# Decoder block on one Trainium2 core: how the key/value banks are emptied, when a gate vector is loaded, and which queue issues some stores

## The chip, the cores and the metric

The kernel runs on one core of one Trainium2 chip. A core has TensorE (PE, matrix products into PSUM banks, with a weight load PEld that overlaps them), VectorE (DVE), ScalarE (ACT), GpSimd (POOL) and SyncE (SP), and 16 DMA engines. Each engine works through its own queue of instructions in order. A DMA is issued by an instruction in the queue of some engine; its transfer then runs beside the engines. The metric is the device time of one execution in microseconds (us), the median of several runs.

## The reference, cut to what matters

One decoder layer over 2048 tokens of width 1024, in fp32. The part that the change touches is the combined projection and what is made of it:

```
h = modulate(rms_norm(x, g_pre_mix), shift_m, scale_m)
proj = h @ w_in
q_a, k_a, v_a, q_m, k_m, v_m, o_m, i_m, f_m, g_a, g_m = split(proj)   # 512 128 128, 4 x 512, 4 4, 2 x 1024
q_a, k_a = rope(q_a, positions), rope(k_a, positions)
y_a = sliding_window_attention(q_a, k_a, v_a, sinks)      # window 128, 8 query heads, 2 key/value heads
y_m = sigmoid(o_m) * head_layer_norm(mlstm_chunkwise(...))
mix = (sigmoid(g_a) * (y_a @ w_branch_attn) + sigmoid(g_m) * (y_m @ w_branch_mlstm)) @ w_out
x = x + gate_m * rms_norm(mix, g_post_mix)
h2 = modulate(rms_norm(x, g_pre_ffn), shift_f, scale_f)
x = x + gate_f * rms_norm((silu(h2 @ w_gate) * (h2 @ w_up)) @ w_down, g_post_ffn)
```

## The kernel before

Every fp32 product is made of three products of a rounded part and a remainder ("hi" and "lo"): ScalarE casts an operand to its hi part (L259 for weights, L1348 in paired products), VectorE subtracts to get the lo part (L260, L1349), and PE multiplies hi by hi, hi by lo and lo by hi (L204). Some large products are paired after Strassen and Winograd, with seven products for eight.

The 2048 tokens are cut into four blocks of 512, each of four subtiles of 128 tokens, and two blocks make a superblock. For a superblock the order of the work is: q and key/value projection of its first block (`q_kv`), attention, the mLSTM value projection (`vm`) of both blocks, `q_kv` and attention of the second block, then pairs for mLSTM q and k, output gate and branch gates, and the outputs. So `q_kv` ends in a key/value group at four places: once before a `vm` group and once before the first pair, in each superblock. The FFN follows (`program2`).

A projection of a block is a `token_group` (L310): four PSUM banks named `acc`, one for each subtile. The weights come in pieces; the last piece finishes the banks one after the other, and `evac(t, ps)` empties each. There are four `acc` banks in all, so that the next group's first matmul for a subtile can't start before the bank has been read by everything that reads it. Four more banks, `mix`, serve transposes and smaller products.

The key/value group is 264 columns wide: 128 of k, 128 of v, 8 gate preactivations (i and f). `evac_kv` reads its bank five times: VectorE adds the gate biases (L801, L802), ScalarE copies v into a buffer (L804), VectorE subtracts the previous subtile's v, `v_last`, from it (L805; the attention product over two neighbouring key tiles uses v and a difference), and `rope` (L746) copies k with ScalarE (L751). Between them ScalarE copies the new `v_last` (L806), which waits for L805. The two stores of v and of the difference go to `at_d` in HBM (L808, L810), from which attention loads them. `rope` multiplies and adds on VectorE (L759 to L763); for k the last addition (L763) is on GpSimd. The stream of a q or k subtile then waits a set delay and transposes, splits and stores (`q_stream` L766, stores L775; `k_stream` L788).

Temporary buffers named `tx` come from one pool of nine (L103), `tm` from another of nine (L106). A new tile waits until all users of the old one, a store from it too, are done.

The order of the instructions on each engine isn't written out by hand. The program issues them in its own order with set delays for the small streams, and the Tile scheduler places them by times of its own; after that the order on each engine is fixed. All DMAs are issued by SP's queue, so a store there stands until its data is made, and later loads stand behind it. Each DMA signals one of eight completion semaphores, which are given out in turn over all queues in the scheduled order; an issue waits for the DMA that had its semaphore before.

The other lines that the change touches: the normalized rows after the mixer (`norm_out` store L561, `residual_out` store L588), the mLSTM value store L823, the attention output store L970 and the mLSTM output store L1089 (a hi and a lo part each), the output gate store L1150, the branch gate store L1160 (where ScalarE has made the stored copy), and `load_gg` (L1809), which loads the vector that scales the FFN's result, at the start of `program2` (L1814). The FFN's first residual sums read the layer's stored rows and L1426 and L1429 build the operands of its first pairs.

Of the kernel before, what the change touches and what calls it, by code (L numbers as in the profile page):

```python
# [10 lines left out]
F32 = mybir.dt.float32  # L11
# [4 lines left out]
ALU = mybir.AluOpType  # L16
# [3 lines left out]
P = 128  # L20
S = 2048
D = 1024
KD = D // P
TB = 512
NT = TB // P
# [6 lines left out]
HQ, HKV, HD = 8, 2, 64  # L32
GQ = HQ // HKV
# [38 lines left out]
def decoder_block(ctx: ExitStack, tc: tile.TileContext, a: dict, out: bass.AP, dbg=None):  # L72
    nc = tc.nc
# [29 lines left out]
    def tx(shape, dtype=F32):  # L103
        return tpool.tile(shape, dtype, tag="tx", name=nm("tx"), bufs=9)
# [106 lines left out]
    def spawn(gen, delay=0.0):  # L211
        st = [now[0] + delay, gen, False]
        streams.append(st)
        return st
# [340 lines left out]
    def norm_out(xy, t, dst_n, sx):  # L555

        V.tensor_tensor(sx[:, 0:1], sx[:, 0:1], sx[:, 1:2], op=ALU.add)
        r = rsqrt_of_sumsq(sx[:, 0:1], 1)
        for xr, y0, c in xy:
            A.activation(y0, xr, AF.Copy, scale=r[:, 0:1])  # L560
            nc.sync.dma_start(dst_n[t * P:(t + 1) * P, c], y0)  # L561

    def residual_out(nk, lhs, w, keep, resid, gg, dst, dst_n):


        st = {}

        def rest(t, y, r):
            ys = (st["keep"][:, t, :], y)
            cs = [slice(h2 * 512, (h2 + 1) * 512) for h2 in range(2)]  # L570
            if dst_n is not None:
                yield L_REST[0] + L_REST[1] * t
            xs = [resid(t, c) for c in cs]
            if dst_n is not None:
                yield L_REST[2]
            sx = small.tile([P, 2], F32, tag="sx", name=nm("sx"), bufs=4)
            for h2 in range(2):
                V.scalar_tensor_tensor(xs[h2], ys[h2], r[:, 0:1], xs[h2], op0=ALU.mult, op1=ALU.add)
                nc.sync.dma_start(dst[t * P:(t + 1) * P, cs[h2]], xs[h2])
                if dst_n is not None:  # L580
                    A.activation(ys[h2], xs[h2], AF.Square, accum_out=sx[:, h2:h2 + 1])
            if dst_n is not None:
                V.tensor_tensor(sx[:, 0:1], sx[:, 0:1], sx[:, 1:2], op=ALU.add)
                r2 = rsqrt_of_sumsq(sx[:, 0:1], 1)
                yield L_REST[3]
                for h2 in range(2):
                    A.activation(ys[h2], xs[h2], AF.Copy, scale=r2[:, 0:1])
                    nc.sync.dma_start(dst_n[t * P:(t + 1) * P, cs[h2]], ys[h2])  # L588

        def evac(hf, t, ps):  # L590
            if not st:
                st["ss"] = small.tile([P, 8], F32, tag="ss8", name=nm("ss8"), bufs=2)
                st["keep"] = keep([NT, 512])
            ss = st["ss"]
            y = st["keep"][:, t, :] if hf == 0 else tm([P, 512])
            A.activation(y, ps, AF.Square, accum_out=ss[:, hf * 4 + t:hf * 4 + t + 1])
            V.tensor_tensor(y, ps, gg(slice(hf * 512, (hf + 1) * 512)), op=ALU.mult)
            if hf == 0:
                return
            s = small.tile([P, 1], F32, tag="ss1", name=nm("ss1"), bufs=4)  # L600
            V.tensor_tensor(s, ss[:, t:t + 1], ss[:, 4 + t:5 + t], op=ALU.add)
            g = rest(t, y, rsqrt_of_sumsq(s, 1, 4.0 * EPS))
            if dst_n is not None:
                spawn(g, next(g))
            else:
                for _ in g:
                    pass

        for hf in range(2):
            yield from token_group(srcs_rows(w, nk, hf * 512), nk, 512, lhs, lambda t, ps, hf=hf: evac(hf, t, ps))  # L610
# [125 lines left out]
    def superblock(sb):  # L736
        b0, b1 = 2 * sb, 2 * sb + 1
        R = {}
# [4 lines left out]
            return lhs  # L743


        def rope(ps, heads, b, t):  # L746
            sin, cos = tables[sb]
            t += (b % 2) * NT
            W = heads * HD
            raw = tx([P, W])  # L750
            A.copy(raw, ps[:, :W])  # L751
            src = raw.rearrange("p (h u f) -> p h u f", u=2, f=32)
            cb = cos[:, t, :].unsqueeze(1).to_broadcast([P, heads * 2, 32])
            sb_ = sin[:, t, :].unsqueeze(1).to_broadcast([P, heads, 32])
            y = tx([P, W])
            z = tx([P, W])
            zz = z.rearrange("p (h u f) -> p h u f", u=2, f=32)
            yy = y.rearrange("p (h u f) -> p h u f", u=2, f=32)
            V.tensor_tensor(y.rearrange("p (h f) -> p h f", f=32), raw.rearrange("p (h f) -> p h f", f=32), cb, op=ALU.mult)  # L759
            V.tensor_tensor(zz[:, :, 0, :], src[:, :, 1, :], sb_, op=ALU.mult)  # L760
            V.tensor_tensor(zz[:, :, 1, :], src[:, :, 0, :], sb_, op=ALU.mult)
            V.tensor_tensor(yy[:, :, 0, :], yy[:, :, 0, :], zz[:, :, 0, :], op=ALU.subtract)
            (G if heads == HKV else V).tensor_tensor(yy[:, :, 1, :], yy[:, :, 1, :], zz[:, :, 1, :], op=ALU.add)  # L763
            return y

        def q_stream(b, t, y):  # L766
            yield L_ROPE
            pt = mix_tile()
            for j in range(GQ):
                transpose(pt[:, j * P:(j + 1) * P], y[:, j * P:(j + 1) * P])  # L770
            hi, lo = tx([P, 512], F32R), tx([P, 512], F32R)
            A.activation(hi, pt, AF.Copy, scale=HD ** -0.5)
            V.scalar_tensor_tensor(lo, pt, HD ** -0.5, hi.bitcast(F32), op0=ALU.mult, op1=ALU.subtract)
            for i, q in enumerate((hi, lo)):
                nc.sync.dma_start(at_d[b * NT + t][:, i * 512:(i + 1) * 512], q.bitcast(F32))  # L775

        R["qk"] = []

        def evac_q(b):
            return lambda t, ps: R["qk"].append(spawn(q_stream(b, t, rope(ps, HQ, b, t))))  # L780

        def load_kv():
            raw = raw_tile([KD, 264])
# [14 lines left out]

        def evac_kv(b):
            def evac(t, ps):  # L800
                V.tensor_tensor(gt[:, t, 0:4], ps[:, 256:260], b_if[:, 0:4], op=ALU.add)  # L801
                V.tensor_tensor(gt[:, t, 32:36], ps[:, 260:264], b_if[:, 4:8], op=ALU.add)  # L802
                va = tx([P, 2, P])
                A.copy(va[:, 0, :], ps[:, 128:256])  # L804
                V.tensor_tensor(va[:, 1, :], ps[:, 128:256], v_last, op=ALU.subtract)  # L805
                A.copy(v_last, va[:, 0, :])  # L806
                n = b * NT + t
                nc.sync.dma_start(at_d[n][:, AT_V + P:], va[:, 1, :])  # L808
                if n + 1 < S // P:
                    nc.sync.dma_start(at_d[n + 1][:, AT_V:AT_V + P], va[:, 0, :])  # L810
                R["qk"].append(spawn(k_stream(b * NT + t, rope(ps, HKV, b, t))))
            return evac

        def q_kv(b):
# [4 lines left out]
        def vm(b):  # L819
            def evac(t, ps):  # L820
                v = tx([P, 512])
                A.copy(v, ps)
                nc.sync.dma_start(vm_d[b][:, t, :], v)  # L823
            yield from token_group(srcs_rows(w_in, KD, C_VM), KD, 512, lhs_h(b), evac)


# [63 lines left out]
        def attention(n):  # L890
# [76 lines left out]
            A.copy(yh, yps)  # L967
            V.tensor_tensor(yl, yps, yh.bitcast(F32), op=ALU.subtract)
            for i, y in enumerate((yh, yl)):
                nc.sync.dma_start(y_d[b][:, i, :, t * P:(t + 1) * P], y.bitcast(F32).rearrange("p (j q) -> p j q", j=GQ))  # L970

        ready = [0]

# [63 lines left out]
        def chunk_out(c):  # L1037
# [48 lines left out]
            A.copy(yh, om)  # L1086
            V.tensor_tensor(yl, om, yh.bitcast(F32), op=ALU.subtract)
            for i, y in enumerate((yh, yl)):
                nc.sync.dma_start(y_d[b][:, 2 + i, :, cs], y.bitcast(F32))  # L1089

        outs = []

# [51 lines left out]
        def done_om(p):  # L1144
            def done(qd, v, in_psum):
                f, b = 2 * p + int(qd[0]) - 1, b0 + int(qd[1]) - 1
                u = plain() if in_psum else v
                A.activation(u, v, AF.Tanh, scale=0.5)
                A.activation(u, u, AF.Identity, scale=om_s[:, f:f + 1], bias=om_s[:, f:f + 1])
                nc.sync.dma_start(om_d[b][:, f, :], u)  # L1150
            return done

        def done_gate(i, p):
            def done(qd, v, in_psum):
                f, b = 2 * p + int(qd[0]) - 1, b0 + int(qd[1]) - 1
                u = v
                if in_psum:
                    u = plain()
                    A.copy(u, v)
                nc.sync.dma_start(g_d[b][:, i, f, :], u)  # L1160
            return done

        def in_pair(kind, p):
# [167 lines left out]
    F = {}  # L1331
# [466 lines left out]
    def program():  # L1798
# [7 lines left out]
        yield lambda: next(phase2)  # L1806
        yield from items[last:]

    def load_gg():  # L1809
        F["gg"] = F["pool"].tile([P, D], F32, name="gg_f")  # L1810
        nc.sync.dma_start(F["gg"], gg_f_d)

    def program2():
        yield load_gg  # L1814
        for b2 in range(NB2):
            yield from gate_up(b2)
            yield from down(b2)

    phase2 = run2(program2())
# [31 lines left out]
```

## Time and profile before

| what | value |
|---|---|
| median of 3 runs | 2741.42 us (2739.41 to 2742.02) |
| profiled execution, own time | 2741.79 us |
| profiled execution, span from first to last instruction | 2740.1 us |
| mean granted PE clock | 0.988 of full speed |
| instructions | 35791 |
| moved by DMA | 513.99 MB, 188 GB/s on average |

The profile gives for each engine its busy time and share of the span. Views of the trace group instructions by the kernel's line, the tile written and the tiles read; `acc<-big,hl` at L204 is a matmul into an `acc` bank. Where a row ends in brackets, as `[8.55 <-ACT tx L751]`, the engine stood idle for that long before the instruction, and what ended it is named: here ScalarE's instruction of L751 that wrote a `tx` tile. An "x4" is four instructions in a row.

A view of stretches gives, for each span of time, the busy time of each engine, the clock that PE was granted (1.00 is full speed) and the share of the DMA engines' time that was used. The trace shows four long waits of PE for L751, at about 86, 208, 776 and 896 us.

### The profile page before, as it was taken

To read this page: it belongs to the slowest core of one execution; us is meant where nothing else is said; L and a number is where in the kernel's file an instruction comes from. 1 tells how busy PE (TensorE), PEld (TensorE's weight loads), DVE (VectorE), ACT (ScalarE), POOL (GpSimd) and SP (SyncE) were. 2 spreads that over 40 slices of the span, in tenths; PEclk is the share of its full clock that TensorE was granted. 3 is DMA by queue.
4 is the path that set the end of the run, shared out by engine and by line. 5 is a ranking of instruction groups with operands and counts; after the bars stand their busy time and mean duration, and the time that the engine had idled before them with its cause. 6 is when DMAs were issued, how large, how long until landed. Compare 5 with 4: busy or idle time off the path is not lost.

```text
span 2740.1 us, 35791 instructions
## 1 busy us (share of the span) xinstructions
PE 2646.6 (97%) x12310; PEld 2139.0 (78%) x12310; DVE 1995.3 (73%) x3922; ACT 1292.4 (47%) x2542; POOL 158.6 (6%) x205
## 2 busy tenths in 40 slices
PE   6898999999989899999998999999999999999998
PEld 4666788888876668888887888888877888888886
DVE  7959877767785988876586767776677766766466
ACT  5646644445754564344563433334554333333444
POOL 2010002100101000110000000000000000000000
PEclk9999999999999999999999999999999999999999
DMA  6655445687674545568755654446675323324566
GB/s 247 232 173 166 139 142 174 212 330 257 218 239 126 199 154 159 185 219 304 255 195 197 198 179 161 147 157 204 208 261 192 116 98 102 108 97 141 183 214 215
DMA packets 355223, 513.99 MB, mean 188 GB/s; under 512 B 25297, under 2 KB 213837, under 8 KB 349921
## 3 DMA queue, kind: packets, MB, share of 16 engines
q1 hardware_dynamic: 355040, 511.71, 56.3%
q8 instruction: 97, 1.59, 0.2%
q14 instruction: 86, 0.70, 0.1%
HBM read 358.17 MB, written 145.06 MB: 184 GB/s over the span
## 4 chain that ended last, share of the span: by engine, by line
PE 80%; DVE 7%; DMA 6%; issue 4%; ACT 2%; SPq 0%; POOL 0%; DVEq 0%; POOLq 0%; ACTq 0%
PE acc L204 57%; PE mix L204 22%; PE mix L209 2%; DVE hl L1349 1%; DVE tm L428 1%; DMA raw<-in_w_ffn_down_dram 1%; DMA big<-big 1%; DMA tx<-in_w_ada_dram 1%; DMA big<-g_d 1%; ACT hl L1348 1%; DVE wlo L260 0%; DMA raw<-as_d 0%; DMA at<-at_d 0%; DMA big<-in_x_dram 0%; ACT tm L941 0%
## 5 line engine op out<-in xcount | busy, mean ns | idle before, releaser
L204 PE MATMUL acc<-big,hl 128*128 128x512 f32 x3936 | 949.5, 395 | 14.9 <-ACT tx L751 13.1
L204 PEld LDWEIGHTS acc<-big,hl 128*128 128x128 f32 x3936 | 735.8, 189 | 184.3 <-ACT tx L751 13.5
L1348 ACT CAST hl<-raw 128x512 fp32r<-128x512 f32 x732 | 440.2, 621 | 488.4 <-PE acc L204 226.7
L1349 DVE TENSOR_TENSOR hl<-raw,hl 128x512 fp32r<-128x512 f32 x732 | 497.9, 696 | 195.9 <-ACT hl L1348 195.4
L204 PE MATMUL acc<-whi,big 128*128 128x512 f32 (+1 forms) x1280 | 382.7, 378 | 22.8 <-ACT tx L751 15.0
L204 PE MATMUL mix<-big,hl 128*128 128x512 f32 x1232 | 334.0, 393 | 8.1 <-DVE big L1429 7.0
L204 PEld LDWEIGHTS acc<-whi,big 128*128 128x128 f32 x1280 | 234.9, 190 | 72.5 <-ACT tx L751 15.9
L204 PEld LDWEIGHTS mix<-big,hl 128*128 128x128 f32 x1232 | 231.7, 188 | 59.9 <-DVE big L1429 7.5
L204 PE MATMUL acc<-wlo,big 128*128 128x512 f32 (+1 forms) x640 | 240.6, 378 | 4.6 <-DVE wlo L260 4.5
L204 PE MATMUL acc<-hl,hl 128*128 128x512 f32 x1008 | 237.0, 393 | 4.3 <-DVE hl L1349 2.4
L204 PEld LDWEIGHTS acc<-hl,hl 128*128 128x128 f32 x1008 | 187.0, 188 | 49.6 <-DVE hl L1349 7.9
L204 PE MATMUL mix<-hl,hl 128*128 128x512 f32 x792 | 183.2, 391 | 2.4 <-ACT hl L1348 1.6
L204 PEld LDWEIGHTS mix<-hl,hl 128*128 128x128 f32 x792 | 147.9, 188 | 36.8 <-ACT hl L1348 3.5
L260 DVE TENSOR_TENSOR wlo<-raw,whi 128x1024 fp32r<-128x1024 f32 (+1 forms) x96 | 110.3, 1149 | 76.1 <-ACT whi L259 70.1
L204 PE MATMUL acc<-big,whi 128*128 128x512 f32 x512 | 155.0, 391 | 1.2 <-ACT whi L259 1.2
L259 ACT CAST whi<-raw 128x1024 fp32r<-128x1024 f32 (+1 forms) x96 | 94.3, 984 | 120.6 <-PE acc L204 116.1
L204 PEld LDWEIGHTS acc<-wlo,big 128*128 128x128 f32 x640 | 122.7, 192 | 28.1 <-DVE wlo L260 6.2
L475 POOL TENSOR_TENSOR rs<-ms,nhalf 128x1 f32<-128x1 f32 (+1 forms) x56 | 42.1, 764 | 1650.6 <-DVE ms L473 1518.7
L204 PE MATMUL acc<-hcT2h,hl 128*128 128x512 f32 x352 | 118.1, 396 | 1.5 <-ACT w L1492 1.5
L204 PE MATMUL mix<-hcT4h,hl 128*128 128x512 f32 x352 | 117.3, 394 | 0.0
L204 PEld LDWEIGHTS acc<-big,whi 128*128 128x128 f32 x512 | 95.6, 188 | 21.2 <-ACT whi L259 1.7
L204 PE MATMUL acc<-big,wlo 128*128 128x512 f32 x256 | 96.4, 392 | 0.1
(333 smaller groups left out, 3392.7 us busy)
## 6 DMA issues: line engine op xcount, KB each, us to landing
raw<-in_w_in_dram SPq DMA_DIRECT2D x48, 1024.0 KB
as_d<-w SPq DMA_DIRECT2D x154, 256.0 KB
raw<-as_d SPq DMA_DIRECT2D x70, 512.0 KB
raw<-in_w_ffn_gate_dram SPq DMA_DIRECT2D x22, 1024.0 KB
raw<-in_w_ffn_up_dram SPq DMA_DIRECT2D x22, 1024.0 KB
raw<-ws_d SPq DMA_DIRECT2D x40, 512.0 KB
tx<-in_w_ada_dram SPq DMA_DIRECT2D x64, 256.0 KB
y_d<-tm SPq DMA_DIRECT2D x64, 256.0 KB
```

What stands on the lines that cost most here:

```text
L204: T.matmul(o, lhsT=lhsT, rhs=rhs, start=start, stop=stop, skip_group_check=resumed)
L209: T.transpose(o, i, ident[:k, :k])
L259: A.copy(hv, src)
L260: V.tensor_tensor(lv, src, hv.bitcast(F32), op=ALU.subtract)
L428: V.scalar_tensor_tensor(acc, raw[:, k, :], c_, acc, op0=ALU.mult, op1=ALU.add)
L475: G.tensor_tensor(r[:, :n], ms[:, :n], nhalf[:, :n], op=ALU.pow)
L1348: A.copy(v(hi), src)
L1349: V.tensor_tensor(v(lo), src, v(hi).bitcast(F32), op=ALU.subtract)
```

## The change

- `evac_kv` copies the whole bank, 264 columns, with one ScalarE operation into a buffer of 392 columns. All else reads that buffer: rope, the subtraction (into the last 128 columns), the gate additions. `v_last` is now copied by VectorE. The two stores read the same buffer. `rope` takes a buffer in place of a bank, and its last addition is on VectorE for k too. `evac_q` makes the copy that `rope` made.
- Stores of what ScalarE has just written are issued by ScalarE's queue (`nc.scalar`) in place of SP's: 128 of them in an execution, by source line 8 (L561), 24 (L588), 16 each of L775, L823, L970, L1089 and L1150, and 16 of L1160's 64. Of a hi and lo pair the hi part moves; the lo part, made by VectorE, stays on SP.
- The gate vector's tile is still placed at the start of `program2`, and its load is yielded after the first `gate_up`.

```diff
         for xr, y0, c in xy:
             A.activation(y0, xr, AF.Copy, scale=r[:, 0:1])
-            nc.sync.dma_start(dst_n[t * P:(t + 1) * P, c], y0)
+            nc.scalar.dma_start(dst_n[t * P:(t + 1) * P, c], y0)
...
-        def rope(ps, heads, b, t):
+        def rope(raw, heads, b, t):
             sin, cos = tables[sb]
             t += (b % 2) * NT
             W = heads * HD
-            raw = tx([P, W])
-            A.copy(raw, ps[:, :W])
+            raw = raw[:, :W]
...
-            (G if heads == HKV else V).tensor_tensor(yy[:, :, 1, :], yy[:, :, 1, :], zz[:, :, 1, :], op=ALU.add)
+            V.tensor_tensor(yy[:, :, 1, :], yy[:, :, 1, :], zz[:, :, 1, :], op=ALU.add)
...
             for i, q in enumerate((hi, lo)):
-                nc.sync.dma_start(at_d[b * NT + t][:, i * 512:(i + 1) * 512], q.bitcast(F32))
+                (nc.scalar, nc.sync)[i].dma_start(at_d[b * NT + t][:, i * 512:(i + 1) * 512], q.bitcast(F32))
...
         def evac_q(b):
-            return lambda t, ps: R["qk"].append(spawn(q_stream(b, t, rope(ps, HQ, b, t))))
+            def evac(t, ps):
+                raw = tx([P, 512])
+                A.copy(raw, ps)
+                R["qk"].append(spawn(q_stream(b, t, rope(raw, HQ, b, t))))
+            return evac
...
         def evac_kv(b):
             def evac(t, ps):
-                V.tensor_tensor(gt[:, t, 0:4], ps[:, 256:260], b_if[:, 0:4], op=ALU.add)
-                V.tensor_tensor(gt[:, t, 32:36], ps[:, 260:264], b_if[:, 4:8], op=ALU.add)
-                va = tx([P, 2, P])
-                A.copy(va[:, 0, :], ps[:, 128:256])
-                V.tensor_tensor(va[:, 1, :], ps[:, 128:256], v_last, op=ALU.subtract)
-                A.copy(v_last, va[:, 0, :])
+                raw = tx([P, 392])
+                A.copy(raw[:, :264], ps[:, :264])
+                v, dv = raw[:, 128:256], raw[:, 264:392]
                 n = b * NT + t
-                nc.sync.dma_start(at_d[n][:, AT_V + P:], va[:, 1, :])
+                y = rope(raw, HKV, b, t)
+                V.tensor_tensor(dv, v, v_last, op=ALU.subtract)
+                V.tensor_copy(v_last, v)
+                V.tensor_tensor(gt[:, t, 0:4], raw[:, 256:260], b_if[:, 0:4], op=ALU.add)
+                V.tensor_tensor(gt[:, t, 32:36], raw[:, 260:264], b_if[:, 4:8], op=ALU.add)
+                nc.sync.dma_start(at_d[n][:, AT_V + P:], dv)
                 if n + 1 < S // P:
-                    nc.sync.dma_start(at_d[n + 1][:, AT_V:AT_V + P], va[:, 0, :])
-                R["qk"].append(spawn(k_stream(b * NT + t, rope(ps, HKV, b, t))))
+                    nc.sync.dma_start(at_d[n + 1][:, AT_V:AT_V + P], v)
+                R["qk"].append(spawn(k_stream(n, y)))
             return evac
...
+    def place_gg():
+        F["gg"] = F["pool"].tile([P, D], F32, name="gg_f")
+
     def load_gg():
-        F["gg"] = F["pool"].tile([P, D], F32, name="gg_f")
         nc.sync.dma_start(F["gg"], gg_f_d)
 
     def program2():
-        yield load_gg
+        yield place_gg
         for b2 in range(NB2):
             yield from gate_up(b2)
+            if b2 == 0:
+                yield load_gg
             yield from down(b2)
```

The other stores that move are edited like the first one above or, where a hi and a lo part are stored in a loop, like the one in `q_stream`.

More of the change, by code (lines that the diff above doesn't have):

```diff
@@ L587, in rest @@
                     A.activation(ys[h2], xs[h2], AF.Copy, scale=r2[:, 0:1])
-                    nc.sync.dma_start(dst_n[t * P:(t + 1) * P, cs[h2]], ys[h2])
+                    nc.scalar.dma_start(dst_n[t * P:(t + 1) * P, cs[h2]], ys[h2])
         def evac(hf, t, ps):
@@ L822, in evac @@
                 A.copy(v, ps)
-                nc.sync.dma_start(vm_d[b][:, t, :], v)
+                nc.scalar.dma_start(vm_d[b][:, t, :], v)
             yield from token_group(srcs_rows(w_in, KD, C_VM), KD, 512, lhs_h(b), evac)
@@ L969, in attention @@
             for i, y in enumerate((yh, yl)):
-                nc.sync.dma_start(y_d[b][:, i, :, t * P:(t + 1) * P], y.bitcast(F32).rearrange("p (j q) -> p j q", j=GQ))
+                (nc.scalar, nc.sync)[i].dma_start(y_d[b][:, i, :, t * P:(t + 1) * P], y.bitcast(F32).rearrange("p (j q) -> p j q", j=GQ))
         ready = [0]
@@ L1088, in chunk_out @@
             for i, y in enumerate((yh, yl)):
-                nc.sync.dma_start(y_d[b][:, 2 + i, :, cs], y.bitcast(F32))
+                (nc.scalar, nc.sync)[i].dma_start(y_d[b][:, 2 + i, :, cs], y.bitcast(F32))
         outs = []
@@ L1149, in done @@
                 A.activation(u, u, AF.Identity, scale=om_s[:, f:f + 1], bias=om_s[:, f:f + 1])
-                nc.sync.dma_start(om_d[b][:, f, :], u)
+                nc.scalar.dma_start(om_d[b][:, f, :], u)
             return done
@@ L1159, in done @@
                     A.copy(u, v)
-                nc.sync.dma_start(g_d[b][:, i, f, :], u)
+                (nc.scalar if in_psum else nc.sync).dma_start(g_d[b][:, i, f, :], u)
             return done
```

## The prediction

> **What bounds the kernel now.** I read the page first: busy time, then the chain that ended last.
>
> ```profile
> span 2740.1 us, 35791 instructions
> ...
> PE 2646.6 (97%) x12310; PEld 2139.0 (78%) x12310; DVE 1995.3 (73%) x3922; ACT 1292.4 (47%) x2542; POOL 158.6 (6%) x205
> ...
> PE 80%; DVE 7%; DMA 6%; issue 4%; ACT 2%; SPq 0%; POOL 0%; DVEq 0%; POOLq 0%; ACTq 0%
> ```
>
> TensorE (PE) is the bound: it stands idle for 2740.1 − 2646.6 = 93.5 us, and no edit here takes a matmul away. So the change can gain only idle time, and what the clock loses after it. The waits of PE, grouped by what ended them, say whose idle time that is; the last row is ScalarE's (ACT) own largest wait.
>
> ```profile
> PE acc L204 <- ACT tx L751: 28.0, 5, 8.6
> PE mix L204 <- DVE big L1429: 7.0, 1, 7.0
> PE mix L204 <- DMA at<-at_d: 2.8, 2, 2.3
> PE mix L204 <- ACT hl L1348: 2.0, 4, 0.8
> PE acc L204 <- ACT whi L259: 1.8, 3, 1.2
> ```
>
> ```profile
> ACT hl L1348 <- PE acc L204: 291.8, 176, 4.4
> ```
>
> The columns are us in total, times, longest. L751 is the copy that empties a key/value bank for rope: 28.0 us in five waits, at four places (site 1 to 4: the two key/value groups of each superblock). Elsewhere ScalarE waits for PE, not PE for ScalarE. Site 1 in order of time, first the stretches (us, busy of PE, PEld, DVE, ACT, POOL, granted PE clock, DMA share, GB/s), then the instructions of ScalarE, VectorE (DVE) and PE:
>
> ```profile
> 88.00:90.00 2.00, 0.00 (x0) 0.00 (x0) 2.00 (x7) 1.98 (x5) 0.00 (x0) 1.00 1.03 390
> 96.00:98.00 2.00, 2.00 (x6) 1.53 (x5) 2.00 (x10) 0.90 (x5) 0.83 (x1) 0.54 0.24 68
> ```
>
> ```profile
> 85.64 0.78 ACT L518 ACTIVATE big<-mix,sh,s 128x512 fp32r<-128x512 f32 x1
> 89.62 0.29 ACT L804 COPY tx<-acc 128x128 f32<-128x128 f32 x1
> 94.12 0.30 ACT L806 COPY v_last<-tx 128x128 f32<-128x128 f32 x1 [0.59 <-DVE tx L805]
> 94.32 0.26 ACT L751 COPY tx<-acc 128x128 f32<-128x128 f32 x1
> ```
>
> ```profile
> 93.80 0.28 DVE L805 TENSOR_TENSOR tx<-acc,v_last 128x128 f32<-128x128 f32 x1
> ```
>
> ```profile
> 94.63 0.80 PE L204 MATMUL acc<-whi,big 128*128 128x512 f32 x1 [8.55 <-ACT tx L751]
> ...
> 100.12 0.62 PE L204 MATMUL acc<-whi,big 128*128 128x512 f32 x2
> ...
> 100.80 0.62 PE L204 MATMUL acc<-whi,big 128*128 128x512 f32 x2
> ...
> 101.48 0.39 PE L204 MATMUL acc<-whi,big 128*128 128x512 f32 x1
> ```
>
> The bank is full at about 86. ScalarE first has six modulate operations (85.64 to 89.62), copies v, and then L806, and L751 behind it, stand behind the subtraction L805, which waits its turn in a VectorE that is busy 2.00 of 2.00 us. Only then may PE start, and it starts at half clock (0.54 in the second stretch). From 94.63 on stand the 24 matmuls of the next group's first piece, 6 for each bank; the last begins at 101.48 and ends near 101.7. At full clock 3 take 0.68 us (100.12 to 100.80), 24 take 5.4, so the half clock costs 7.1 − 5.4 = 1.7 us. The other three sites show the same chain (PE, then ScalarE):
>
> ```profile
> 216.49 2.07 PE L204 MATMUL acc<-big,hl 128*128 128x512 f32 x4 [8.34 <-ACT tx L751]
> 780.86 0.79 PE L204 MATMUL acc<-whi,big 128*128 128x512 f32 x1 [3.90 <-ACT tx L751]
> 900.55 3.65 PE L204 MATMUL acc<-big,hl 128*128 128x512 f32 x9 [4.71 <-ACT tx L751]
> ```
>
> ```profile
> 209.52 2.16 ACT L551 CAST big<-big 128x512 fp32r<-128x512 f32 x4
> 215.97 0.30 ACT L806 COPY v_last<-tx 128x128 f32<-128x128 f32 x1 [4.13 <-DVE tx L805]
> 774.63 0.28 ACT L804 COPY tx<-acc 128x128 f32<-128x128 f32 x1
> ...
> 780.37 0.28 ACT L806 COPY v_last<-tx 128x128 f32<-128x128 f32 x1
> 895.99 0.25 ACT L804 COPY tx<-acc 128x128 f32<-128x128 f32 x1
> 900.03 0.30 ACT L806 COPY v_last<-tx 128x128 f32<-128x128 f32 x1 [0.21 <-DVE tx L805]
> ```
>
> From the first copy to the second the bank is held 4.5, 4.4, 5.7 and 4.0 us, by VectorE's queue.
>
> **Part 1, the banks.** The change removes three ScalarE copies of 128 columns for each of 16 subtiles and adds one of 264. Only wider and narrower copies are in the trace:
>
> ```profile
> L751 ACT COPY tx<-acc x32: 253/418/624, 65.8 to 909.6; 128x512 f32<-128x512 f32 x16, 128x128 f32<-128x128 f32 x16
> ```
>
> The new one lies between 0.25 and 0.62 us; I take 0.4, half way, so ScalarE saves about 16 x (0.27 + 0.30 + 0.26 − 0.4) = 7 us, none of it on the path. What counts is that the bank no longer waits for VectorE. What is late next is the buffer the copy goes to. It holds v and dv until their two stores have landed, and it comes from the pool of nine that the q streams use. I followed the changed kernel's order on each engine, which is fixed before it runs, against the times above.
>
> Site 1: the copies of subtiles 0 and 1 now stand ahead of the six modulate operations (about 85), the third behind them, waiting for a q store too (about 91), the fourth for VectorE's rope of subtile 0 (about 95). The 24 matmuls then end at 95 + 6 x 0.23 = 96.4 instead of 101.7. Gain 5.3; bounds 0, and 8.6 of idle with 1.7 of half clock.
> Site 2: the first copy stands behind eight casts (ending 211.7) and a store that lands near 212; PE starts near 213 instead of 216.5, still long enough idle for the clock to fall. Gain 3.4, bounds 0 and 10.
> Site 3 (two waits, 28.0 − 8.55 − 8.34 − 4.71 = 6.4 together): copies near 775.5, 777 and 778.6, the fourth near 785, when subtile 0's stores have landed. PE starts at about 776.5 instead of 780.9. Its order gives the first three banks two pieces, 36 matmuls or 8.2 us, before the fourth, so it gets there at 784.7 and loses up to 1 us; with no long gap the clock stays up, worth site 1's 1.7 at most. Gain 3.9 − 1 + 1.6 = 4.5, bounds 0 and 8.1.
> Site 4: copies near 895.5 and 897.5, where the order gives PE 2.8 us of work on the first before the second, so it loses at most 1 us instead of 4.7, and keeps the clock, which in the row below cost half of 2 us. Gain 4.7 − 1 + 1.0 = 4.7, bounds 0 and 6.4.
>
> ```profile
> 901.00:903.00 2.00, 2.00 (x6) 1.52 (x6) 2.00 (x8) 1.17 (x3) 0.34 (x1) 0.50 0.82 212
> ```
>
> Sum −5.3 − 3.4 − 4.5 − 4.7 = −17.9, bounds 0 and −35 (28.0 us, and 4 x 1.7 of half clock).
>
> A rule stands beside these rows. The Trainium skill, "TensorE: Matmul & The Clock Gate", Part 1, says that PE falls to half clock after an idle window of about 3.4 us and needs about as long a busy one to return. The trace agrees (0.54 in the second stretch at site 1, two us after the restart). By that rule site 2, still idle for 5 us, keeps its penalty, and sites 3 and 4 lose theirs; without it the sum would be 1.6 + 1.0 smaller, −13.3, and the time 2728.1.
>
> **Part 2, the stores.** 128 of the stores move from SP's queue to ScalarE's. Their issue cost is known from SP only:
>
> ```profile
> L775 SPq DMA_DIRECT2D at_d<-tx x32: 319/400/1325, 76.0 to 896.6; - x32
> L1150 SPq DMA_DIRECT2D om_d<-tx x16: 319/320/383, 260.5 to 1019.2; - x16
> L1089 SPq DMA_DIRECT2D y_d<-tm x32: 359/385/2136, 427.3 to 1268.1; - x32
> ```
>
> At medians of 0.32 to 0.40 us this is 41 to 51 us of ScalarE, of which it has 2740.1 − 1292.4 idle. What hides it is that ScalarE's splits run ahead of PE: it waits 291.8 us at L1348 alone. Without that cover each issue costs its 0.4 us. An issue also waits for the store's own copy, and for an earlier transfer that used the same completion semaphore; behind it wait ScalarE's casts, and PE for those. Against the landing times of before nearly all of these have landed; a few wait 0.7 to 2.5 us. Bounds: 0, and 51. PE's waits for ScalarE's casts are 2.0 and 1.8 us in 2740, the nearest row, and I take as much again, +2.
>
> SP loses waits, since it no longer stands behind ScalarE's results; the largest of them:
>
> ```profile
> SPq L1150 <- ACT tx L1149: 53.3, 15, 10.6
> ```
>
> Loads behind them issue sooner, but PE waits for such a load (at_d) only 2.8 us: I take −0.5, bounds +1 and −2.8.
>
> A rule speaks against this part. The Trainium skill, "Trainium Kernel Development and Optimization", Key Constraints, says that queues of several engines share the same 16 DMA engines, so that a second issuer saves issue time alone. The trace has one issuer, but shows a DMA share of 1.03 at site 1; by the rule no store lands sooner, and my sum counts none that does.
>
> **Part 3, VectorE.** It gains a copy of v_last (128 columns) and the rope addition that GpSimd did. The nearest row is L805's 0.28; 16 x 0.5 = 8 us at most, lying in stretches where VectorE is full and what it owes comes later. PE waits for VectorE little there; I take +1, bounds 0 and 8.
>
> **Part 4, the gate vector.** Its load is yielded later, but in the changed order it still stands right behind the first gate weights and ahead of the loads that PE waits for. Only its wait is gone: it no longer stands behind the last residual store.
>
> ```profile
> 1446.00:1450.00 4.00, 0.00 (x0) 0.00 (x0) 0.39 (x1) 0.00 (x0) 0.00 (x0) 0.51 0.96 333
> ```
>
> PE is idle here for 7.0 us (the L1429 row), but the transfers fill the DMA engines (0.96), so issuing sooner brings little: −0.5, bounds 0 and −3.4 (its wait).
>
> **Sum.** −17.9 + 2 − 0.5 + 1 − 0.5 = −15.9. The profiled execution took 2741.79 us (span 2740.1 and 1.7 around it), 0.4 above the median 2741.42. So the median should come to 2741.4 − 15.9 = 2725.5.
>
> **Rivals.**
> All banks free in time: the buffers come back sooner than I reckon, no site idles over 3.4 us. Then −35 + 2 and 2708. For it: ScalarE has idle time at every site. Against: the third and fourth copy wait for stores while DMA shares are near 1.
> The wait changes its name: the copy waits for its buffer as long as it did for VectorE (the change doesn't do what it says). PE's 28.0 us stay, ended by the new copy; with +2 from the other parts 2743.4. For it: two of my four sites have the fourth bank near the old time. Against: the first two have no such wait.
> ScalarE becomes the bound of the path: in-order issues hold its casts. Without its +2 the sum is −17.9, so the point from which it decides is where 17.9 of up to 51 us of issue reach PE, about a third. If half does, 2741.4 − 17.9 + 25.5 = 2749, slower. One place is most open to it: a store at site 4 waits for a 1 MB load's semaphore just before the copies, near 892 to 897. For it: issues of 1.3 and 2.1 us at the far end. Against: the 291.8 us for which ScalarE waits.
>
> **How the numbers follow.** Forecast 0.55, with a range of its own of 2716 to 2735; banks all free 0.12; wait renamed 0.16; ScalarE bound 0.17. A measurement of this kernel tells about 0.2% (5.5 us) from no change: faster 0.67, same 0.16, slower 0.17. The range takes in the renamed wait and ends at the two outer rivals: 2708 to 2750.
>
> **What would show it.** In the waits of PE, L751's 28.0 us should fall to about 10 to 14 under the new copy's line, site 2 the longest (about 5); the clock in the stretches after sites 3 and 4 should stay at 1.00. PE's waits for L1348 and L259 should stay under 6 us together, and L1429's near 7. If ScalarE's waits for PE shrink by far more than 50 us while PE's for its casts grow, the third rival holds. The forecast is wrong if the fourth copies come much later than 95 and 785.

## The result, and the profile after

The changed kernel takes 2748.91 us (median of 20 runs, 2743.42 to 2753.17) against 2742.90 us for the kernel before, measured beside it (20 runs). The ratio is 1.0018, with a 95% interval of 1.0011 to 1.0024: 3 to 7 us slower, where 16 us faster was forecast. Ratios here are the recorded ones of undisturbed executions (one of e16, at 11225 us, is left out), and differ a little from quotients of the medians. One kernel's executions lie up to 14 us apart, and a profile is of one execution, often not a median one: the change's took 2745.93 us, e9's 2738.47 where its median is 2733.49, e17's 2737.68 where its median is 2732.44. So a difference of a few us between two profiles is read only where a row names its place.

The page of the kernel after (line numbers from here on are those of the changed kernel):

```profile
span 2744.2 us, 35664 instructions
...
PE 2648.2 (97%) x12310; PEld 2138.6 (78%) x12310; DVE 1997.5 (73%) x3954; ACT 1289.2 (47%) x2510; POOL 149.4 (5%) x189
...
PE 78%; DVE 10%; DMA 7%; ACT 3%; issue 2%; SPq 1%; POOL 0%; ACTq 0%; DVEq 0%; POOLq 0%
```

PE's idle time is 96.0 us where it was 93.5, so what the banks gave back was lost elsewhere. PE's waits (us in total, times, longest), where L805 is now the copy of the whole key/value bank:

```profile
PE acc L204 <- ACT tx L805: 9.0, 5, 4.0
PE acc L204 <- ACT tx L827: 7.6, 2, 5.7
...
PE mix L209 <- POOL tm L950: 6.9, 7, 2.3
PE mix L204 <- DVE big L1434: 5.8, 1, 5.8
...
PE acc L204 <- ACT tx L781: 4.1, 2, 2.4
...
PE mix L204 <- ACT tm L959: 3.2, 2, 2.9
...
PE mix L204 <- ACT hl L1353: 2.1, 3, 1.4
...
PE acc L204 <- ACT hl L1353: 1.8, 3, 0.7
...
PE acc L204 <- ACT whi L259: 0.9, 1, 0.9
```

The 28.0 us are now 9.0. In their place stand waits that were not there or were small: L827, the copy of the mLSTM value banks, 7.6; L950, the attention's normalization, 6.9 (1.4 before); L959, its copy of transposed weights, 3.2 (0.4 before).

The first site, ScalarE and then PE:

```profile
83.73 0.67 ACT L805 COPY tx<-acc 128x264 f32<-128x264 f32 x2
...
90.25 0.38 ACT L805 COPY tx<-acc 128x264 f32<-128x264 f32 x1 [0.54 <-DMA at_d<-tx]
93.06 0.38 ACT L805 COPY tx<-acc 128x264 f32<-128x264 f32 x1 [2.44 <-DVE tx L762]
```

```profile
90.68 0.50 PE L204 MATMUL acc<-whi,big 128*128 128x512 f32 x1 [1.46 <-ACT tx L805]
```

The copies come at 84, 90.3 and 93.1, as worked out (85, 91, 95), and PE waits 1.5 us instead of 8.6. But the same group of value matmuls ends in a new hole, 27 us later. PE, ScalarE, and a stretch behind them (busy PE, PEld, DVE, ACT, POOL, clock, DMA share, GB/s):

```profile
117.36 0.79 PE L204 MATMUL acc<-whi,big 128*128 128x512 f32 x1 [5.67 <-ACT tx L827]
```

```profile
114.65 2.18 ACT L551 CAST big<-big 128x512 fp32r<-128x512 f32 x4 [2.06 <-DMA big<-big]
116.73 1.06 ACT L827 COPY tx<-acc 128x512 f32<-128x512 f32 x2
```

```profile
118.00:120.00 2.00, 2.00 (x6) 1.59 (x5) 2.00 (x6) 0.00 (x0) 0.00 (x0) 0.50 0.94 311
```

The copies L827 stand behind four casts L551, and these wait for a transfer of `big`. After 5.7 us of idle the clock is down again. What site 1 had won is gone.

### The profile page after: what moved, and what is told of

Same layout as the page of the kernel before. It is cut to its first block, busy times and chain, and to the rows that moved or that the text cites. A ratio compares the mean times of both kernels' runs of the same rounds, so it can differ in the third digit from the quotient of the medians.

```text
span 2744.2 us, 35664 instructions
## 1 busy us (share of the span) xinstructions
PE 2648.2 (97%) x12310; PEld 2138.6 (78%) x12310; DVE 1997.5 (73%) x3954; ACT 1289.2 (47%) x2510; POOL 149.4 (5%) x189
## 4 chain that ended last, share of the span: by engine, by line
PE 78%; DVE 10%; DMA 7%; ACT 3%; issue 2%; SPq 1%; POOL 0%; ACTq 0%; DVEq 0%; POOLq 0%
PE acc L204 55%; PE mix L204 21%; DVE hl L1354 2%; PE mix L209 2%; DVE tm L428 1%; DMA raw<-as_d 1%; ACT hl L1353 1%; DMA w<-x 1%; DMA tx<-in_w_ada_dram 1%; DVE tx L1132 1%; DMA ws_d<-big 1%; DMA raw<-in_w_ffn_down_dram 1%; DMA raw<-ws_d 0%; ACT tm L946 0%; DMA at_d<-tx 0%
## 5 line engine op out<-in xcount | busy, mean ns | idle before, releaser
L1353 ACT CAST hl<-raw 128x512 fp32r<-128x512 f32 x732 | 440.0, 621 | 484.9 <-PE acc L204 224.8
L259 ACT CAST whi<-raw 128x1024 fp32r<-128x1024 f32 (+1 forms) x96 | 94.2, 983 | 127.1 <-PE acc L204 106.3
```

The source lines that it names most:

```text
L259: A.copy(hv, src)
L1353: A.copy(v(hi), src)
```

## The experiments

Two theories at first. Theory 1: the banks come free as meant, and an order that the edits shifted gives the gain back elsewhere. Theory 2: the stores on ScalarE's queue eat the gain. Each kernel was timed in five rounds beside the kernel before; all ratios are to it.

| kernel | median us | ratio, 95% interval |
|---|---|---|
| the whole change | 2748.91 | 1.0018 (1.0011 to 1.0024) |
| e1 banks alone | 2731.70 | 0.9953 (0.9937 to 0.9969) |
| e2 stores alone | 2741.78 | 0.9995 (0.9985 to 1.0005) |
| e3 before, other order | 2746.31 | 1.0005 (0.9995 to 1.0015) |
| e4 change, L551 on GpSimd | 2742.43 | 0.9993 (0.9983 to 1.0003) |
| e5 banks and stores | 2747.18 | 1.0008 (1.0000 to 1.0017) |
| e6 banks and gate vector | 2732.09 | 0.9957 (0.9945 to 0.9969) |
| e7 change, other order | 2747.37 | 1.0015 (1.0006 to 1.0025) |
| e8 banks, other order | 2735.24 | 0.9968 (0.9956 to 0.9980) |
| e9 banks, 16 q stores | 2733.49 | 0.9966 (0.9955 to 0.9978) |
| e10 change, q stores on SP | 2736.34 | 0.9979 (0.9971 to 0.9988) |
| e11 change, second copy held | 2741.67 | 0.9995 (0.9986 to 1.0005) |
| e12 banks, 80 late stores | 2734.51 | 0.9967 (0.9954 to 0.9979) |
| e13 banks, value and attention stores | 2741.85 | 0.9997 (0.9987 to 1.0007) |
| e14 change, q and attention stores on SP | 2737.98 | 0.9981 (0.9973 to 0.9990) |
| e15 banks, L551 on GpSimd | 2739.91 | 0.9989 (0.9979 to 0.9999) |
| e16 as e15, gate vector later | 2737.89 | 0.9983 (0.9974 to 0.9992) |
| e17 banks, value stores | 2732.44 | 0.9963 (0.9949 to 0.9978) |
| e18 banks, attention stores | 2729.55 | 0.9948 (0.9935 to 0.9960) |

### One part at a time: e1, e2, e3, e4

e1 has the edits of `rope`, `evac_q` and `evac_kv` only:

> Only the key/value bank part of the change; all stores stay on SP, the gate vector's load as before. Theory 1 (a wait moved: the banks come free as meant, and the gain of some 20 us is given back later, where PE meets operations that a new order has put ahead of what it needs): the waits for the bank copies are near 17 us as in the changed kernel, new waits elsewhere sum to as much as was gained, and the time is 2738 to 2750, as with the whole change. Theory 2 (the stores on ScalarE's queue eat the gain): the bank part alone is faster than before by 15 us or more, 2728 or less.

e2 has the moved stores only, all 128:

> Only the 128 stores on ScalarE's queue; the banks are emptied as before. Theory 1: within 5 us of before, 2738 to 2748, with L751's wait still near 28 us. Theory 2: slower than before by 10 us or more, 2753 and up, with ScalarE's casts (L1348, L259) late for PE.

e3 changes one planned delay of the kernel before:

```diff
-L_SOFT, L_PT, L_PV = 8000.0, 1300.0, 1000.0
+L_SOFT, L_PT, L_PV = 8300.0, 1300.0, 1000.0
```

> The kernel before with one number of its order's planning changed (the set delay ahead of the attention's transposes, 8000 to 8300), so that the same instructions stand in a slightly different order. Theory 1 needs that order alone can move waits: the time differs from before by 2 us or more either way, and PE's waits change in stretches where nothing was done. Theory 2 does not need it: within 1 us of before.

e4 is the whole change with:

```diff
-                A.copy(hi[:, k, :], v)
+                G.tensor_copy(hi[:, k, :], v)
```

> The changed kernel, with the hi casts of the summed blocks (L551) on GpSimd in place of ScalarE, so that they no longer stand ahead of the mLSTM value copies (L827) on ScalarE. Theory 1: PE's wait of 5.7 us for L827 near 117 us falls under 1.5 us and the stretch from 85 to 125 us gains about 6 us; the whole is 2 to 8 us faster than the changed kernel unless order takes it elsewhere. Theory 2: the wait stays, since a store's issue and not the casts holds ScalarE.

The bank part alone is 0.9953, about 13 us faster: theory 1 in its first form falls, since it expected no gain. Theory 2 has its prediction for e1 nearly met (2728 or less) and fails on e2: the stores alone cost nothing. e3 is within noise and tells nothing. e4 is 6 us faster than the change, as theory 1 said, but PE's wait for L827 fell only to 3.8 us; with the casts out of the way the copy stood for its buffer:

```profile
114.69 0.59 ACT L827 COPY tx<-acc 128x512 f32<-128x512 f32 x1 [2.29 <-DMA at_d<-tx]
```

So the cast is not all that comes late: a store that holds a `tx` buffer lands near 114.6. The trace names one of L813, the stores of the value difference.

### Which parts cost together: e5, e6, e7, e8

e5 leaves the gate vector's edit out of the change, e6 adds only that edit to the banks, e7 and e8 put e3's delay into the change and into the bank part.

> The bank part and the stores on ScalarE's queue, without the later gate vector. The bank part alone gave 2731.7, the whole change 2748.9, the stores alone 2741.8. Theory A (the two parts cost together: ScalarE's queue holds stores where the bank copies stand): near the whole change, 2744 to 2752. Theory B (order alone: any edit shuffles the planned order and moves waits by several us): anywhere from 2728 to 2750, and its losses stand at other places than those of the whole change. Theory C (the gate vector's edit, which moves no work, shuffles the order to the bad one): near the bank part alone, 2729 to 2735.

> The bank part and the later gate vector, all stores on SP. Theory A: near the bank part alone, 2729 to 2735. Theory B: anywhere from 2728 to 2750. Theory C: near the whole change, 2744 to 2752.

> The whole change, with the set delay ahead of the attention's transposes 8300 in place of 8000, so that the order shifts and no work changes. Theory A: stays near the whole change, 2744 to 2753, since the issues stand in ScalarE's queue in any order. Theory B: differs from it by 4 us or more, with the waits near 117 and 271 us changed. Theory C: says nothing of it.

> The bank part alone, with the same delay at 8300. Theory A and C: stays near the bank part alone, 2728 to 2735. Theory B: differs from it by 4 us or more.

The times fit theory A in all four, in e8 0.2 us past its edge; its reason, stores that stand in ScalarE's queue, isn't shown by times. Stores beside the banks cost 15.5 us (2747.18 against 2731.70), and the gate vector's edit costs nothing. The shifted delay moves 3.5 us at most (e8), less than theory B's 4, though it does move single waits. One is the attention's wait near 271 us, which the change has; the same stretch of e7 has only 1.2 us for L1353:

```profile
PE mix L209 <- POOL tm L950: 3.6, 3, 2.3
```

e7 is no faster for it: that wait comes and goes with the planned order, and taking it away did not take the loss away.

### Number or place: e9, e10, e11, e12

The next question was whether the stores cost by their number (issue time on ScalarE) or by what they displace. Compare SP's queue in the change and in e1 (start, us, instruction):

```profile
100.63 0.56 SPq L545 DMA_DIRECT2D big<-big  x1
...
103.20 1.22 SPq L290 DMA_DIRECT2D raw<-in_w_in_dram  x1
104.55 0.75 SPq L545 DMA_DIRECT2D big<-big  x1
...
107.23 0.48 SPq L813 DMA_DIRECT2D at_d<-tx  x1
107.77 3.91 SPq L800 DMA_DIRECT2D at_d<-tx  x3
```

```profile
99.51 0.56 SPq L545 DMA_DIRECT2D big<-big  x1
...
105.33 0.50 SPq L813 DMA_DIRECT2D at_d<-tx  x1
105.88 2.84 SPq L800 DMA_DIRECT2D at_d<-tx  x3
...
115.52 0.60 SPq L545 DMA_DIRECT2D big<-big  x1
```

In e1 the second 1 MB copy L545 is issued at 115.5, after the key stores L800. In the change it goes at 104.6, ahead of six of the eight and of the last two stores of the value difference (L813). A 1 MB weight load stands ahead of these in both kernels (103.20, and 102.22 in e1), so that the one copy L545 is the difference. e4 has the change's order here: its last store L813 is issued at 106.67, 1.3 us later than in e1, but in e1 the first value copy gets its buffer 4.7 us sooner:

```profile
109.98 0.59 ACT L827 COPY tx<-acc 128x512 f32<-128x512 f32 x1 [3.54 <-DMA at_d<-tx]
```

e9 is e1 with L774's edit of the diff, e10 the change without it, e12 is e1 with the store edits of L561, L588, L1094, L1155 and L1165. e11 keeps every store on ScalarE and holds the second copy back (`mark` is a tile of one element):

```diff
                 A.copy(v, ps)
+                if b == b0 and t == 0:
+                    A.copy(mark, v[0:1, 0:1])
                 nc.scalar.dma_start(vm_d[b][:, t, :], v)
...
             lo = hc_part(name, 1)
+            if name == "T4":
+                A.copy(lo[0:1, 0, 0:1], mark)
             nc.sync.dma_start(lo.bitcast(F32), raw)
```

> The bank part, and of the 128 stores only the 16 of q (L774) on ScalarE's queue. Theory P (place: with the q stores off SP's queue the planned order issues a second 1 MB copy, L545, ahead of the key stores near 104 us; these land late, hold buffers, and the mLSTM value copies L827 wait): nearly half of the loss of all stores, 2737 to 2742, with PE's wait for L827 near 4 to 6 us. Theory N (number: each issue on ScalarE costs its share, 15.5 us / 128 = 0.12 us): 16 of them cost 2 us, 2731 to 2735, and no wait for L827 over 2 us.

> The whole change with the 16 q stores (L774) left on SP's queue, so that the second L545 stands behind the key stores again. Theory P: 2738 to 2743, and the loss between the key/value group and the end of the value group near 120 us is gone. Theory N: 2746 to 2749.

> The whole change, all 128 stores on ScalarE, with the second 1 MB copy (L545, T4) made to wait for the first mLSTM value copy: two ScalarE copies of one element are added, one that marks the copied value and one that writes the mark into the copy's target. Lines below the edit are 3 to 5 higher. Theory P: PE's wait of 5.7 us near 117 us falls under 2 us; 2739 to 2744. Theory N: 2748 to 2751, as the issues stay.

> The bank part, and on ScalarE's queue only the 80 stores outside the projection and attention stage (L561, L588, L1094, L1155, L1165); L774, L828 and L975 stay on SP. Theory P: 2731 to 2736, the 2 us near 575 to 585 us being all that is lost. Theory N: 80 x 0.12 = 10 us, 2739 to 2743.

The second L545 is issued at 106.85 in e9, 115.75 in e10 and 117.52 in e11 (L548 there). PE's wait for the value copy in the stretch from 80 to 125 us, in this order (e11's lines are shifted):

```profile
PE acc L204 <- ACT tx L827: 5.2, 1, 5.2
```

```profile
PE acc L204 <- ACT tx L827: 1.3, 1, 1.3
```

```profile
PE acc L205 <- ACT tx L830: 1.5, 1, 1.5
```

So 16 moved stores bring the wait, and either putting them back or holding one copy takes most of it away, with all 128 on ScalarE in e11. For this one wait, place is shown. The buffer is not all of it: in e11 the first value copy still stands for a store until 113.5 (109.98 in e1), but the casts L551 no longer stand ahead of it. e12 moves 80 stores; its 2.8 us beside e1 are within noise, where number said 10, so number falls.

A miss: e9 came to 2733.5 where place said 2737 to 2742. Its profiled execution, with the wait, is one of its two slowest and takes 2738.5; whether its faster ones have the wait is not known. And e10 beat its range by 2 us.

How much of the loss this wait makes is not shown. The medians of e11 and e10 lie 7 and 13 us below the change's. Their profiled executions lie 2.3 and 6.9 us below, and they win this elsewhere. The table counts PE's 12310 matmuls in order of their start (their order differs a little between kernels):

| start of matmul number, us | e1 | change | e10 | e11 |
|---|---|---|---|---|
| 462 (behind the wait) | 120.5 | 125.3 | 122.0 | 123.0 |
| 1988 | 446.0 | 456.0 | 451.3 | 450.9 |
| 6560 (ahead of the FFN's first pairs) | 1388.0 | 1401.4 | 1401.4 | 1404.2 |
| 6824 (behind them) | 1456.0 | 1470.5 | 1465.1 | 1467.4 |
| 12304 | 2719.7 | 2733.9 | 2726.6 | 2731.6 |

Ahead of the FFN, e10 and e11 have lost again what they had won on the change. They win 5 to 6 us at its first pairs, where PE's wait for L1434 is 5.8 us in the change and 0.8 and 0.7 in them. The order on PE differs there. In the change, first, the product that waits stands ahead of the next group's matmuls; in e10 24 of these stand ahead of it:

```profile
1451.83 2.93 PE L204 MATMUL mix<-big,hl 128*128 128x512 f32 x6 [5.83 <-DVE big L1434]
1454.56 3.99 PE L204 MATMUL acc<-big,hl 128*128 128x512 f32 x14
```

```profile
1447.17 5.73 PE L204 MATMUL acc<-big,hl 128*128 128x512 f32 x24 [0.68 <-ACT w L1503]
...
1454.41 2.17 PE L204 MATMUL mix<-big,hl 128*128 128x512 f32 x8 [0.82 <-DVE big L1434]
```

No edit asks for this order; e2 and e9 have it too (waits of 0.5 and 1.5 us). So it came with the plan, by luck.

### The rest: e13 to e18

Left was the fourth site. There PE waits in the change for the attention's copy L959, behind two groups of casts; in e1 the copy stands between them (ScalarE of the change, PE of the change, ScalarE of e1, PE of e1):

```profile
889.63 2.17 ACT L551 CAST big<-big 128x512 fp32r<-128x512 f32 x4
...
892.78 2.18 ACT L551 CAST big<-big 128x512 fp32r<-128x512 f32 x4
894.86 1.06 ACT L959 COPY tm<-mix 128x512 f32<-128x512 f32 x2
```

```profile
895.49 1.41 PE L204 MATMUL mix<-tm,at 128*64 128x512 f32 x2 [2.92 <-ACT tm L959]
```

```profile
878.40 2.18 ACT L551 CAST big<-big 128x512 fp32r<-128x512 f32 x4
880.49 0.58 ACT L959 COPY tm<-mix 128x512 f32<-128x512 f32 x1
```

```profile
881.12 1.07 PE L204 MATMUL mix<-tm,at 128*64 128x512 f32 x2 [0.80 <-ACT tm L959]
```

e13 is e1 with the edits of L828 and L975, e14 the change without those of L774 and L975, e17 and e18 are e1 with one of L828 and L975 each. e15 is e1, and e16 is e6, with e4's edit.

> The bank part, and on ScalarE's queue the 16 mLSTM value stores (L828) and the 16 hi stores of the attention output (L975). The fourth site (second key/value group of the second superblock, its last matmul to the first of the next pair) takes 11 us with the bank part alone and 17 us with the whole change. Theory S (these two kinds of store move the casts L551 and the q splits ahead of the copies that PE waits for there): 15 us or more at the fourth site, and 2735 to 2740 in all. Theory Q (the q stores do that too): 11 to 12 us there, and 2731 to 2735.

> The whole change with the q stores (L774) and the attention output stores (L975) left on SP. Theory S: the fourth site returns to 11 to 13 us and the time to 2732 to 2736. Theory Q: it stays at 15 us or more, as with the q stores alone on SP (2736.3).

> The bank part alone, with the hi casts L551 on GpSimd. If these casts stand ahead of copies that PE waits for in this order too, 2726 to 2730; if the bank part's order has them out of the way already (as its waits near 117 us say), 2730 to 2735.

> The same with the later gate vector. As the gate vector alone moved nothing beside the bank part (2732.1 against 2731.7), within 3 us of the run without it, either way.

> The bank part, and only the 16 mLSTM value stores (L828) on ScalarE's queue. Together with the attention stores they cost 10 us (2741.9 against 2731.7) and put both groups of casts L551 ahead of the two attention copies L959 at the fourth site (PE waits 2.9 us there instead of 0.8). If the value stores do it: 2737 or more and the wait of 2.9 us; if the attention stores do it: 2730 to 2735 and a wait under 1.5 us; if each has a share, 2735 to 2738.

> The bank part, and only the 16 hi stores of the attention output (L975) on ScalarE's queue: the counterpart. If the attention stores do it: 2737 or more and the wait of 2.9 us for L959 at the fourth site; if the value stores do it: 2730 to 2735 and under 1.5 us.

The wait for L959 around the fourth site (860 to 905 us) in e13, e14, e17 and e18:

```profile
PE mix L204 <- ACT tm L959: 2.9, 1, 2.9
```

```profile
PE mix L204 <- ACT tm L959: 0.8, 1, 0.8
```

```profile
PE mix L204 <- ACT tm L959: 1.1, 1, 1.1
```

```profile
PE mix L204 <- ACT tm L959: 1.4, 2, 0.9
```

Both kinds together bring the wait in e13 and cost 10 us beside e1 (2741.9, above theory S's 2735 to 2740); each alone brings neither: 2732.4, and 2729.6, the lowest median of all, though not told apart from e1's. Each of the two results clears its own store and points at the other; none of the cases written for e17 and e18 had both. In the medians, the cost of the stores is therefore not a sum over stores. But the wait does not account for the 10 us. It is less than 2 us longer in e13 than in e17, and the profiled executions of these two, 2738.56 and 2737.68 us, hardly differ. Nor do both kinds of store suffice for it: e11 has both on ScalarE, and its wait for this copy (L964 there) is 0.9 us.

In e14 the wait is gone and the time is no better than e10's (a miss; it expected 2732 to 2736). e15 is 8 us slower than e1, where 2735 at most was expected, and e16 lies within 3 us of it, as expected. So an edit that takes work off ScalarE and moves no store costs about as much as one that adds stores. In its trace, e15 loses 7.4 us to e1 between the 1095th and the 1229th matmul (255 to 286 us in e1), the stretch of the attention's wait near 271 us; the change loses 6.3 there.

## Why the prediction was wrong

**Part 1, the banks, was right in its mechanism and high in its sum.** The copies are in the rows above, and alone with VectorE's share the part gives 0.9953, 9 to 17 us, against −17.9 + 1 = −16.9, at the edge of the interval. In e1's trace PE's waits for the bank copies fall from 28.0 to 8.7 us, but all of PE's idle time falls only from 93.5 to 88.2 and the span by 10.1: other waits take part of the gain back even with no store moved, and the sum had no term for that. The new copy takes 0.38 us (0.4 taken). At site 2 PE still idles, as worked out (4.0 us, where about 5 was expected):

```profile
214.74 8.31 PE L204 MATMUL acc<-big,hl 128*128 128x512 f32 x24 [4.01 <-ACT tx L805]
```

and the clock is at 0.50 behind it (217 to 219 us), while site 3 keeps its clock (786 to 788 us), both as the rule of the Trainium skill ("TensorE: Matmul & The Clock Gate", Part 1) had it:

```profile
217.00:219.00 2.00, 2.00 (x6) 1.57 (x5) 2.00 (x8) 0.13 (x1) 0.00 (x0) 0.50 1.02 383
...
786.00:788.00 2.00, 2.00 (x10) 1.62 (x10) 2.00 (x9) 2.00 (x5) 0.00 (x0) 1.00 0.90 189
```

Site 4, where at most 1 us of wait and a kept clock were expected, has 1.3 us and 1.00 in e1. In the change it has 3.1 us, and the clock is at 0.50 from 897 to 901 us, behind the attention's wait of 2.9.

**Part 2, the stores, is the step that failed.** It gave them +2 and −0.5 us. Beside the banks they cost 15.5 us, and alone nothing (0.9985 to 1.0005). Its cost of an issue was right (median 0.33 to 0.38 us on ScalarE's queue), and so was what hides it: ScalarE's largest wait for PE is still 288.3 us, where it was 291.8, and PE's waits for L1353 and L259 sum to 4.8, under the 6 named. Wrong was the step that freed loads can only help, or cost 1 us at most ("bounds +1 and −2.8"). In its place the runs showed that a load which SP may issue sooner is also a 1 MB transfer ahead of small stores, and the buffers of these stores are what the next copies need: PE's wait for L827 near 117 us is 5.7 us in the change, 1.5 with that copy held and 0.6 in e1. The prediction followed the changed order only at the four sites and against the landing times of before; the second L545 and the casts L551, which that order had moved already, stood outside.

**Part 3** is inside e1 and was not measured by itself. **Part 4, the gate vector,** was put at −0.5, and 2732.1 beside 2731.7 can't be told from nothing.

**The rivals.** "ScalarE becomes the bound" named 2749 and a slower kernel, and the time came out at 2748.9, but not by its mechanism: its own sign, ScalarE's waits for PE shrinking by far more than 50 us while PE waits for casts, isn't there, and 80 stores cost 2.8 us, within noise. That the number agrees is luck. One such hold is in the trace, small: a store's issue waits for an earlier store's landing, and the next cast with it. From the 2582nd to the 2806th matmul, around it, the change loses 2.5 us to e1, and e12 loses 2.9.

```profile
571.30 0.60 ACT L1091 CAST tm<-tm 128x512 fp32r<-128x512 f32 x1
574.09 0.37 ACTq L1094 DMA_DIRECT2D y_d<-tm  x1
574.50 1.05 ACT L259 CAST whi<-raw 128x1024 fp32r<-128x1024 f32 x1 [2.60 <-DMA g_d<-tx]
```

"The wait changes its name" was nearest in kind, but looked for the new name at the same bank, not at the next one. The rival that fits the wait near 117 us was missing: the gain at a site is given back at the next in-order queue that a moved transfer has delayed.

**What stays open.** That moved stores and new banks cost 15.5 us together is shown; where these stand is shown only in part. In the two profiled executions the change is 4.8 us behind e1 at the 462nd matmul (120 us in e1), 10.0 at the 1988th (446), 12.4 at the 2806th (606), 16.2 at the 4226th (900, behind the fourth site), 13.3 at the 6560th and 14.2 at the end. Experiments tie the first of these to the copy that moved up (e9 to e11), and the step near 600 us to the late stores (e12). The attention's stretch and the fourth site are open, and so is why value and attention stores cost 10 us together and nothing apart. Since e15 loses 8 us without a moved store, a changed planned order, brought by any edit, is a rival that remains for them.

## What to carry to other kernels

Moving stores to another queue does not only move their issue: everything behind them moves up, and a large load that moves up can delay small stores whose buffers are needed sooner. So follow each freed queue to the next big transfer, and each won stall to the next in-order wait, before adding up. Where a scheduler sets the order, run parts of a change one by one: here 32 of the 128 stores cost 10 us and either 16 of them nothing, and the bank part alone (0.9953), or with the attention stores (0.9948), beats both kernels. And before a won wait is taken for a won time, compare where the two traces stand further on: e11 removed its wait, and its profiled execution won its time elsewhere.

## What the runs showed of the hardware

A DMA issue on ScalarE's queue takes what it takes on SP's: 0.326 us against 0.319 for the shortest of the q stores, 0.377 against 0.370 at the median of the attention stores (L975). On ScalarE the issues stand in order with the engine's own work, as the cast at 574.50 above shows, which came 2.6 us late behind one. The q stores on both queues (shortest, median, longest in ns; first and last start in us):

```profile
L774 ACTq DMA_DIRECT2D at_d<-tx x16: 326/327/348, 75.8 to 907.0; - x16
L774 SPq DMA_DIRECT2D at_d<-tx x16: 319/348/2064, 79.4 to 908.1; - x16
```

Of the q stores the long ones, up to 2.1 us, are SP's, and the longest on ScalarE's took 0.35. ScalarE's queue has long ones too: a value store (L828) took 1.15 us there, where the median is 0.33.
